# LRU branch ahead of GLA, one more Strassen pair, and other places for scans and cover, in a one-core encoder kernel

## The chip, the cores and the metric

One core of a Trainium2 chip runs the whole program. The metric is the time of one execution on the device in microseconds (us). The profile is of one execution; its span runs from the first instruction to the last. TensorE's matmul queue is called PE, VectorE DVE, ScalarE ACT; SP is the engine whose queue issues most transfers (DMA).

## What the kernel computes

784 tokens (16 meta tokens, 512 and 256 others) of width 2048 are normalised and projected by `w_in`. Three branches work on the columns, each runs over the tokens in both directions, and three sets of 2048 sigmoid gates merge them:

```python
cols = h @ w_in
u_a, gate_a, q_b, k_b, v_b, gate_b, glr_b, x_c, gate_c, merge = split_cols(cols)
y_a = s5_mixer(u_a, ...) * silu(gate_a)             # diagonal state space, 512 wide
y_b = gla_mixer(q_b, k_b, v_b, glr_b, ...) * silu(gate_b)   # gated attention in chunks, 4 heads
y_c = rglru_mixer(x_c, ...) * silu(gate_c)          # convolution, gates, scan, 1024 wide
gates = sigmoid(merge).reshape(bsz, length, 3, D_MODEL)
m = (gates[:, :, 0] * (y_a @ w_out_a) + gates[:, :, 1] * (y_b @ w_out_b)
     + gates[:, :, 2] * (y_c @ w_out_c))
return z + m @ w_o                                  # then a last rmsnorm
```

## The kernel before

Activations lie transposed: 16 tiles of 128 features by 784 tokens, each as a high part `h` and a low part `l` (names h_102, l_103 and so on). Weights are split likewise: `load_w` loads half a tile of 128 outputs (`raw`, 512 KB, two buffers), ACT copies the high part `hi` (L89), DVE subtracts for the low part `lo` (L61); `hi` and `lo` have three buffers each. Every product takes three matmuls (h·hi, l·hi, h·lo), for each half of the tokens. One output tile is thus 96 matmuls (16 x 3 x 2).

The order of the program is: start and projections of S5, branch S5, branch GLA, branch LRU, a Strassen phase (`strassen`, L1138) that computes merge gates and the branch gates in pairs of tiles, and the merge with the output products. The Strassen phase has 8 pairs for the branch gates and `NST` pairs for merge gates; a pair costs 168 matmuls for 2 tiles.

The other 48 - 2 `NST` tiles of merge gates are computed plainly, and most serve as filler for PE: `fill_step` (L273) does 6 of a tile's 96 matmuls and loads weights ahead, `cover(n)` does n such steps where it is called, and `tick` does them at a rate that `pace` sets. The rate is zero in GLA, LRU and behind them, so only `cover` fills there. What is left of the plain tiles is done at the head of `strassen`, between the calls of `sums`.

`sums(k)` (k from 0 to 7) loads two tiles (`xa` and `x`, two buffers each) of the normalised input from `xnorm` and forms the three sums of quadrants that Strassen's products need (`sh`, `sl`); `last_sum(k)` forms a fourth in the place of h and l. The loads for k = 0 and 1 are issued on ACT's queue, the others on SP's. The first products of the Strassen phase use the sums of k = 0 and 1.

In LRU, eight blocks n go through `conv`, `gates` (24 matmuls, L1051), `decays` and `scans`. Two blocks share the changes of ACT's function tables, so `decays` and `scans` are issued for a pair of blocks after each odd n. In GLA, `keys` and `queries` are projections (L199), the decays of a pair of heads come from the small matrix `glr` and the weights `wup` (L791), and attention ends with L916; normalisation of the heads follows (L935, sums over a tile of ones).

A scheduler in the framework sets the order of instructions on each engine when the kernel is built. On the chip each engine then runs in that order and waits where it must.

Of the kernel before, what the change touches and what calls it, by code (L numbers as in the profile page):

```python
# [6 lines left out]
F32 = mybir.dt.float32  # L7
# [7 lines left out]
NM, NP_, NS = 16, 512, 256  # L15
T = NM + NP_ + NS
# [3 lines left out]
HT = T // 2  # L20
# [3 lines left out]
SCRATCH = 1024  # L24
AHEAD = 6
SPLITN = 12
NST = 15
NA = 3
PREP = 6
WH = 3  # L30
PN = (1, 2)
XS = 2
LT = 39
MERGE0 = 36
GATES = [4, 5, 6, 7, 16, 17, 18, 19, 28, 29, 30, 31, 32, 33, 34, 35]
NG2 = len(GATES) // 2
# [59 lines left out]
def build(tc, A, out_p, out_s):  # L96
# [16 lines left out]
    first = S.dma_start(small[:], A["small"])  # L113
# [28 lines left out]
    psA = tc.alloc_tile_pool(name="psA", bufs=4, space=PSUM)  # L142
# [67 lines left out]
    def position(ci):  # L210

        return ci - sum(g < ci for g in GATES)
# [18 lines left out]

    merges = list(enumerate(MERGES[:48 - 2 * NST]))
    def merge_tile():
        i, (d, b) = merges.pop(0)
        merge_out(proj(MERGE0 + i, NM), d, b)
# [138 lines left out]
    ws = [load_w(A["w_in"][position(MERGE0), :, hk * 8:(hk + 1) * 8, :]) for hk in range(2)]  # L374
    for k in range(SPLITN, 16):
        normalise(k)
    pm = [bank(psA, "pm") for h in range(2)]
# [12 lines left out]
    E = dict(locals())  # L390
    branch_s5(E)
    pace(6)
    rates = lru_rates(V, col, cst, gp)
    first = branch_gla(E)
    pace(7)
    branch_lru(E, first, *rates)
    yh, yl = strassen(E)
    gp.release()

# [9 lines left out]
def branch_s5(E):  # L409
    tc, A = E["tc"], E["A"]  # L410
    V, S, PE, SP = E["V"], E["S"], E["PE"], E["SP"]
    col, split, proj, tick, pace, psB, drm, ident, ud = (E[k] for k in (
        "col", "split", "proj", "tick", "pace", "psB", "drm", "ident", "ud"))
# [5 lines left out]
        out=o, in0=x, scalar1=s1, scalar2=s2, op0=o0, **({"op1": o1} if o1 is not None else {}))  # L419
# [111 lines left out]
    for i in range(2):  # L531
        for j in range(4):
            d = 1 - j // 2
            a = Ap[:, 8, i, d * NG:(d + 1) * NG]
# [134 lines left out]
    for q in range(63):  # L669
        if q < 31:  # L670
            advance(33 + q, 34 + q, 1, 3)
        elif q == 31:
            advance(33 + q, 34 + q, 1, 2)
        else:
            advance(q - 31, q - 30, 0, 3)
        tick()
    pace(3)
    for e in range(NE):
        if e + 2 < NE:
# [10 lines left out]
    for n in range(4):  # L690
# [7 lines left out]
        t = fp.tile([128, NT], F32, name="ft")  # L698
# [6 lines left out]
        h = fp.tile([128, NT], F32R, name=f"fh{n}", bufs=1)  # L705
# [8 lines left out]
    for m in range(4):  # L714
# [6 lines left out]
        for h in range(2):  # L721
            sl = slice(h * HN, (h + 1) * HN)
            ps = psB.tile([128, 512], F32, name="br")
# [10 lines left out]
    fp.release()  # L734


def branch_gla(E):
    tc, A = E["tc"], E["A"]
    V, S, PE, SP = E["V"], E["S"], E["PE"], E["SP"]
    col, split, proj, evac, tick, psB = (E[k] for k in ("col", "split", "proj", "evac", "tick", "psB"))  # L740
# [11 lines left out]
    def tmp():  # L752
        return lp.tile([128, T], F32, name="tmp", bufs=4)

    qsp, qip, am = [], [], []
    for i in range(2):
        t = lp.tile([128, 2, 2, 128], F32, name=f"qsp{i}")
        V.memset(t[:], 0.0)
        qsp.append(t)
        t = lp.tile([128, 2, 2, 128], F32, name=f"qip{i}")  # L760
        V.memset(t[:], 0.0)
        qip.append(t)
        t = lp.tile([128, 2, 2, 128], F32, name=f"am{i}")
# [4 lines left out]
    def keys(hp):  # L768
        t = lp.tile([128, T], F32, name="kk")
        evac(t[:], proj(10 + hp, 0), 0)  # L770
        return t

    def queries(hp):
        t = lp.tile([128, NT], F32, name="qq")
        evac(t[:], proj(8 + hp, NM), NM, scale=0.125)
        return t

    kk, qq = keys(0), queries(0)
    S.table("natural_log_exp_and_others")
    for hp in range(2):  # L780

# [3 lines left out]
        for d in range(2):  # L785
            ab = tmp()
            zm = tmp()
            for h in range(2):
                sl = slice(h * HT, (h + 1) * HT)
                ps = psB.tile([128, 512], F32, name="br")  # L790
# [24 lines left out]
        for h in range(2):  # L815
            for g0, blks in ((0, (0, 1, 2, 3)), (4, (4, 5, 6))):
                ps = psB.tile([128, 512], F32, name="br")
# [13 lines left out]
        dec = lp.tile([128, 2, NTL], F32, name="dec")  # L831
        S.activation(out=dec[:, 0, :], in_=bc[:, 0, 143:T:128], func=AF.Exp, scale=IG)
        S.activation(out=dec[:, 1, :], in_=bc[:, 1, 16:T:128], func=AF.Exp, scale=IG)
        for d in range(2):
# [12 lines left out]
            ps = psB.tile([128, 512], F32, name="br")  # L847
# [4 lines left out]
            if d == 0:  # L852
                ps = psB.tile([128, 512], F32, name="br")
                PE.transpose(ps[:16, 0:128], kd[:, 0:16], ident[:])
                S.copy(out=kt[:16, 4, :], in_=ps[:16, 0:128])
                ps = psB.tile([128, 512], F32, name="br")
# [6 lines left out]
            for b in order:  # L863
                ps = psB.tile([128, 512], F32, name="br")
                PE.matmul(ps[:, :256], kt[:, reg.index(b), :], vt[:, b, :, :], start=True, stop=True)
                t = b - 1
# [14 lines left out]
        for t in range(NTL):  # L881
            qs, qi, a = qsp[it % 2], qip[it % 2], am[it % 2]
# [37 lines left out]
        for h in range(2):  # L920
            o = oo[:, h, :]
            sq = tmp()[:, :NT]
            S.activation(out=sq[:], in_=o, func=AF.Square)
            if hp == 0 and h == 0:
                kk = keys(1)
            elif hp == 0:
                qq = queries(1)
            elif h == 0:
                first = proj(20, 0)
            v = tmp()[:, :NT]  # L930
            r = tmp()[:, :NT]
            for i in range(2):
                sl = slice(i * HN, (i + 1) * HN)
                ps = psB.tile([128, 512], F32, name="br")
                PE.matmul(ps[:, :HN], ones[:], sq[:, sl], start=True, stop=True)  # L935
                V.tensor_scalar(out=v[:, sl], in0=ps[:, :HN], scalar1=1.0 / 128, scalar2=EPS,
                                op0=ALU.mult, op1=ALU.add)
            S.activation(out=r[:], in_=v[:], func=AF.Ln)
            S.activation(out=r[:], in_=r[:], func=AF.Exp, scale=-0.5)
            E["rsqrt_newton"](r[:], v[:], sq[:])  # L940
            V.scalar_tensor_tensor(out=o, in0=o, scalar=col("gla_g", 2 * hp + h), in1=r[:], op0=ALU.mult, op1=ALU.mult)
            S.dma_start(E["hspill"][4 + 2 * hp + h], o)
            tick()
    lp.release()
    return first


def exp_acc(V, out, x, r, k, ki):
# [36 lines left out]
    return cp, cn  # L985


def branch_lru(E, first, cp, cn):
    tc, A = E["tc"], E["A"]
    V, S, PE, SP = E["V"], E["S"], E["PE"], E["SP"]  # L990
    col, split, proj, evac, tick, psB = (E[k] for k in ("col", "split", "proj", "evac", "tick", "psB"))
    psA = E["psA"]
    XW, CW, HC = 808, 804, 402

    ws = []

    def load_half(ci, hk):

        if ci < 28:
            ws.append(E["load_w"](A["w_in"][E["position"](ci), :, hk * 8:(hk + 1) * 8, :]))  # L1000
        elif hk == 0:
            E["fill_ahead"]()

    def half(ps, hk):
        E["proj_mm"](ps, *ws.pop(0), hk, 0, HT)

    lp = tc.alloc_tile_pool(name="lp", bufs=1, reuse_waits="tile")

# [63 lines left out]
    def scans(n, gate, a):  # L1072
        for d in range(2):
            gi = gate[2 * d + 1]
            V.tensor_tensor(out=gi[:], in0=gi[:], in1=gate[2 * d][:], op=ALU.mult)
            if d == 0:
                hf = lp.tile([128, CW], F32, name="hf")
                for lo, hi in ((0, 528), (531, 803)):
                    V.tensor_tensor_scan(out=hf[:, lo:hi], data0=a[0][:, lo:hi], data1=gi[:, lo:hi], initial=0.0,
                                         op0=ALU.mult, op1=ALU.add)  # L1080
            else:
                hb = lp.tile([128, NT], F32, name="hb", bufs=2)
                for lo, hi, o in ((16, 528, 0), (547, 803, 512)):
                    V.tensor_tensor_scan(out=rev(hb[:, o:o + hi - lo]), data0=rev(a[1][:, lo:hi]),
                                         data1=rev(gi[:, lo:hi]), initial=0.0, op0=ALU.mult, op1=ALU.add)
            tick()
        V.tensor_tensor(out=hb[:, :512], in0=hb[:, :512], in1=hf[:, 16:528], op=ALU.add)
        V.tensor_tensor(out=hb[:, 512:], in0=hb[:, 512:], in1=hf[:, 547:803], op=ALU.add)
        S.dma_start(E["hspill"][8 + n], hb[:])

    load_half(21, 0)
    ready = conv(0, first)
    pair = []
    for n in range(8):
        if n < 7:
            ps = [E["bank"](psA, "pm") for h in range(2)]
            half(ps, 0)
            load_half(21 + n, 1)
        if n % 2 == 0:
            S.table("sigmoid_and_others")  # L1100
        pair.append((n, gates(n, *ready)))
        if n < 7:
            half(ps, 1)
            load_half(22 + n, 0)
            ready = conv(n + 1, ps)
        if n == 7:
            E["cover"](LT)
        if n % 2:
            S.table("exp_and_others")
            dec = [decays(m, g) for m, g in pair]  # L1110
            S.table("sqrt_and_others")
            for m, g in pair:
                for d in (0, 2):
                    S.activation(out=g[d][:], in_=g[d][:], func=AF.Sqrt)
            for (m, g), a in zip(pair, dec):
                scans(m, g, a)
            pair = []
    lp.release()


def weight_sums(V, r, t):
# [427 lines left out]
def strassen(E):  # L1549
# [78 lines left out]
    xp = tc.alloc_tile_pool(name="stu", bufs=1, reuse_waits="tile")  # L1628
    for i in range(NG2 + NST):
        ps = {j: next_bank() for j in (1, 2, 3, 6, 7, 5, 4)}  # L1630
        for sb in range(4):
            products(PE, ps, ahead.pop(0), sb, 8, operand)
            n = 4 * i + sb + 1
            if n > 2 and n < 4 * (NG2 + NST):
                ahead.append(weights(*divmod(n, 4)))
# [6 lines left out]
        if i < NG2:  # L1642
# [9 lines left out]
            continue  # L1652
        for g, (d, b) in zip((g1, g2), MERGES[48 - 2 * NST + 2 * (i - NG2):]):
            S.dma_start(E["gspill"][d, :, b, :], g[:])
# [29 lines left out]
def layout(inp):  # L1684
# [7 lines left out]
    order = [36 + 16 * b + d for d, b in MERGES]  # L1692
    std = order[:48 - 2 * NST]
    D["w_in"] = np.ascontiguousarray(w3[[i for i in range(36) if i not in GATES] + std])
    pairs = GATES + order[48 - 2 * NST:]
    st = []
# [88 lines left out]
```

## Time and profile before

| what | value |
|---|---|
| median of 3 runs | 2044.0 us (2043.46 to 2046.32) |
| the profiled execution | 2045.25 us, its span 2043.4 us |
| PE busy | 2005.7 us (98%) |
| DVE busy | 1503.8 us (74%) |
| ACT busy | 806.7 us (39%) |
| mean granted clock of TensorE | 0.995 of full |

Busy shares are shares of the span. The profile gives the end of a matmul longer than the distance to the next one, since matmuls overlap; so what PE needs for a run of them is read from start to start.

### The profile page before, as it was taken

To read this page: it belongs to the slowest core of one execution; us is meant where nothing else is said; L and a number is where in the kernel's file an instruction comes from. 1 tells how busy PE (TensorE), PEld (TensorE's weight loads), DVE (VectorE), ACT (ScalarE), POOL (GpSimd) and SP (SyncE) were. 2 spreads that over 40 slices of the span, in tenths; PEclk is the share of its full clock that TensorE was granted. 3 is DMA by queue.
4 is the path that set the end of the run, shared out by engine and by line. 5 is a ranking of instruction groups with operands and counts; after the bars stand their busy time and mean duration, and the time that the engine had idled before them with its cause. 6 is when DMAs were issued, how large, how long until landed. Compare 5 with 4: busy or idle time off the path is not lost.

```text
span 2043.4 us, 30984 instructions
## 1 busy us (share of the span) xinstructions
PE 2005.7 (98%) x12228; PEld 1975.6 (97%) x12228; DVE 1503.8 (74%) x2784; ACT 806.7 (39%) x1172; POOL 0.2 (0%) x4
## 2 busy tenths in 40 slices
PE   8999989999999999999999999999999999999997
PEld 8999989999999999999999999999999999999997
DVE  8988983746567875876776656655669989887778
ACT  7332111433437765433333222222235435533345
POOL 0000000000000000000000000000000000000000
PEclk9999989999999999999999999999999999999999
DMA  8652224521211223533443233323356335532256
GB/s 292 253 120 93 75 91 117 173 65 34 75 34 63 90 83 108 181 125 113 135 134 111 88 104 103 104 88 104 104 176 221 124 112 182 173 120 94 94 162 218
DMA packets 105378, 252.12 MB, mean 123 GB/s; under 512 B 18960, under 2 KB 39952, under 8 KB 105232
## 3 DMA queue, kind: packets, MB, share of 16 engines
q1 hardware_dynamic: 77072, 200.61, 30.6%
q10 hardware_dynamic: 28160, 49.53, 6.8%
q8 instruction: 96, 1.57, 0.3%
q14 instruction: 50, 0.41, 0.1%
HBM read 200.65 MB, written 49.45 MB: 122 GB/s over the span
## 4 chain that ended last, share of the span: by engine, by line
PE 86%; DVE 9%; ACT 3%; DMA 2%; issue 0%; SPq 0%; DVEq 0%; ACTq 0%
PE pm L1138 24%; PE br L1138 23%; PE pm L199 13%; PE pm L273 9%; PE br L1411 4%; PE pm L1281 2%; PE br L1281 2%; DVE sc L61 2%; PE pm L332 2%; DVE W L61 2%; PE br L1051 1%; DVE lo L61 1%; DMA c<-gspill 1%; PE br L199 1%; PE pm L1411 1%; ACT gt L89 1%
## 5 line engine op out<-in xcount | busy, mean ns | idle before, releaser
L89 ACT ACTIVATE hi<-raw 128x768 fp32r<-128x768 f32 (+2 forms) x234 | 216.0, 923 | 493.1 <-PE br L1138 131.5
L61 DVE TENSOR_TENSOR lo<-raw,hi 128x768 fp32r<-128x768 f32 (+2 forms) x234 | 246.1, 1053 | 141.2 <-ACT hi L89 141.1
L61 DVE TENSOR_TENSOR lo<-t,hi 128x1024 fp32r<-128x1024 f32 x140 | 171.4, 1224 | 193.9 <-ACT hi L89 193.8
L89 ACT ACTIVATE hi<-t 128x1024 fp32r<-128x1024 f32 x140 | 148.4, 1060 | 281.7 <-PE pm L1138 135.4
L1138 PE MATMUL pm<-l,hi 128*128 128x384 f32 (+1 forms) x616 | 197.3, 320 | 0.0
L1138 PE MATMUL pm<-h,hi 128*128 128x384 f32 (+1 forms) x616 | 196.6, 319 | 0.0
L1138 PE MATMUL pm<-h,lo 128*128 128x384 f32 (+1 forms) x616 | 196.6, 319 | 0.0
L1138 PE MATMUL br<-l,hi 128*128 128x384 f32 (+1 forms) x504 | 167.0, 331 | 0.0
L1138 PE MATMUL br<-h,hi 128*128 128x384 f32 (+1 forms) x504 | 165.9, 329 | 0.0
L1138 PE MATMUL br<-h,lo 128*128 128x384 f32 (+1 forms) x504 | 165.8, 329 | 0.0
L199 PE MATMUL pm<-h,hi 128*128 128x392 f32 (+1 forms) x608 | 162.2, 345 | 1.2 <-ACT xp L1020 1.2
L199 PE MATMUL pm<-h,lo 128*128 128x392 f32 (+1 forms) x608 | 159.1, 341 | 2.5 <-DVE lo L61 2.5
L199 PE MATMUL pm<-l,hi 128*128 128x392 f32 (+1 forms) x608 | 159.7, 341 | 0.0
L273 PE MATMUL pm<-h,hi 128*128 128x384 f32 x512 | 134.1, 343 | 0.0
L273 PE MATMUL pm<-h,lo 128*128 128x384 f32 x512 | 132.1, 339 | 2.1 <-DVE lo L61 2.1
L273 PE MATMUL pm<-l,hi 128*128 128x384 f32 x512 | 132.6, 340 | 0.0
L1138 PEld LDWEIGHTS pm<-h,hi 128*128 128x128 f32 x616 | 115.7, 188 | 0.4 <-ACT h L89 0.2
L1138 PEld LDWEIGHTS pm<-h,lo 128*128 128x128 f32 x616 | 116.0, 188 | 0.0
L1138 PEld LDWEIGHTS pm<-l,hi 128*128 128x128 f32 x616 | 115.7, 188 | 0.0
L199 PEld LDWEIGHTS pm<-h,lo 128*128 128x128 f32 x608 | 111.2, 188 | 2.8 <-DVE lo L61 2.8
L199 PEld LDWEIGHTS pm<-h,hi 128*128 128x128 f32 x608 | 111.1, 188 | 2.8 <-ACT xp L1020 1.5
L199 PEld LDWEIGHTS pm<-l,hi 128*128 128x128 f32 x608 | 110.6, 188 | 0.2
(358 smaller groups left out, 4802.2 us busy)
## 6 DMA issues: line engine op xcount, KB each, us to landing
raw<-in_w_st SPq DMA_DIRECT2D x92, 512.0 KB
raw<-in_w_in SPq DMA_DIRECT2D x74, 512.0 KB
gspill<-g ACTq DMA_DIRECT2D x48, 384.0 KB
raw<-in_w_ost SPq DMA_DIRECT2D x32, 512.0 KB
xr<-in_xT SPq DMA_DIRECT2D x31, 392.0 KB
m<-gspill SPq DMA_DIRECT2D x26, 384.0 KB
raw<-in_w_out SPq DMA_DIRECT2D x16, 512.0 KB
raw<-in_w_outc SPq DMA_DIRECT2D x16, 512.0 KB
```

The lines of the kernel that those rows point to most:

```text
L61: return f(*a, **k)
L89: ins = self.eng.activation(**k)
L199: PE.matmul(ps[h][:, :nw], w[:, k, :], xx[kt][:, n0 + h * nw:n0 + (h + 1) * nw], start=(kt == 0 and j == 0), stop=(kt == 15 and j == 2))
L273: PE.matmul(ps[h][:, :HN], w[:, k % 8, :], xx[k][:, NM + h * HN:NM + (h + 1) * HN], start=(k == 0 and j == 0), stop=(k == 15 and j == 2))
L332: PE.matmul(ps0[2 * t + h][:, :HT], w[:, k, :], xx[kt][:, h * HT:(h + 1) * HT], start=(kt == 0 and j == 0), stop=(kt == 15 and j == 2))
L1051: PE.matmul(ps[:, :HC], w[:, gs], xx[:, sl], start=(j == 0), stop=(j == 2))
L1138: PE.matmul(ps[j][:, :nt], w[:, wi, kk, :], x, start=(k == 0 and q == 0), stop=(k == n - 1 and q == 2))
L1281: PE.matmul(ps[h][:, :HN], w[:, 4 * b + k, :], yy[4 * b + k][:, h * HN:(h + 1) * HN], start=(k == 0 and j == 0), stop=(k == 3 and j == 2))
L1411: PE.matmul(po[:, :NS], x[:, n, :], y[k][:, ss], start=(first and j == 0), stop=(last and j == 2))
```

## The change

Branch LRU runs ahead of GLA. `NST` goes from 15 to 16. LRU's last block, which had 39 steps of cover (`LT`) behind it, gets GLA's first keys and queries instead (`next_branch`, 192 matmuls into tiles of a pool `kq`); GLA's last head, which had LRU's first projection (96 matmuls) beside it, gets `cover(16)` (also 96). LRU's first projection `proj(20, 0)` is now called at its own start. In S5, `cover(6)` (36 matmuls) is called behind the loop of `advance`. In LRU the scans of a pair of blocks are issued one at a time: the first after the odd block, the second after the next even one.

```diff
-NST = 15
+NST = 16
-LT = 39
...
-    first = branch_gla(E)
+    kq = tc.alloc_tile_pool(name="kq", bufs=1)
+    first = branch_lru(E, kq, *rates)
     pace(7)
-    branch_lru(E, first, *rates)
+    branch_gla(E, *first)
+    kq.release()
     yh, yl = strassen(E)
...
         tick()
+
+    E["cover"](6)
     pace(3)
...
-    kk, qq = keys(0), queries(0)
...
             elif h == 0:
-                first = proj(20, 0)
+                E["cover"](16)
...
+    def next_branch():
+
+        out = []
+        for i, (ci, n0, scale) in enumerate(((10, 0, 1.0), (8, NM, 0.125))):
+            ps = [E["bank"](psA, "pm") for h in range(2)]
+            load_half(ci, 1)
+            half(ps, 0, n0)
+            if i == 0:
+                load_half(8, 0)
+            half(ps, 1, n0)
+            t = kq.tile([128, T - n0], F32, name=("kk0", "qq0")[i])
+            evac(t[:], ps, n0, scale=scale)
+            out.append(t)
+        return out
...
+    first = proj(20, 0)
     load_half(21, 0)
     ready = conv(0, first)
...
         if n == 7:
-            E["cover"](LT)
-        if n % 2:
+            first = next_branch()
+        if n % 2 == 0:
+            scan_one()
+        else:
...
-            for (m, g), a in zip(pair, dec):
-                scans(m, g, a)
+            due = [(m, g, a) for (m, g), a in zip(pair, dec)]
+            scan_one()
             pair = []
+    scan_one()
```

Two places in the order of instructions carry most of what changes beside that.

The first is SP's queue where GLA's small inputs are loaded: `glr`, the masks and `wup`, among the loads of weights (`raw`). Before:

```order
L716 DMA fw<-in_w_glu 128x512 x2
L135 DMA raw<-in_w_in 128x1024 x4
L748 DMA glr<-glrd 64x784
L750 DMA masks<-in_gla_mask 128x256
L783 DMA wup<-in_gla_up 128x2x128
L135 DMA raw<-in_w_in 128x1024 x3
```

The same with the change, where `gw` are the weights of LRU's gates:

```order
L1038 DMA gw<-in_lru_w 128x512
L134 DMA raw<-in_w_in 128x1024 x7
L751 DMA glr<-glrd 64x784
L753 DMA masks<-in_gla_mask 128x256
L785 DMA wup<-in_gla_up 128x2x128
L134 DMA raw<-in_w_in 128x1024
```

The three loads now stand behind the seven weight loads that end LRU; the last two of these (named raw_6113 and raw_6425 in the full listing) take their buffers over from weights whose `lo` stands behind LRU's last scan on DVE.

The second is ACT's queue ahead of the Strassen phase, where `xa` and `x` for the first `sums` are loaded (`hb` is a result of LRU's scans, `g<-pm` empties a finished filler tile). Before:

```order
L1089 DMA hspill<-hb 128x768
L89 ACTIVATE g<-pm 128x384 x2
L89 ACTIVATE hi<-raw 128x1024
L240 DMA gspill<-g 128x768
L1089 DMA hspill<-hb 128x768
L1570 DMA xa<-xnorm 128x768
L1570 DMA x<-xnorm 128x384
L1570 DMA xa<-xnorm 128x768
L89 ACTIVATE hi<-raw 128x1024
L1570 DMA x<-xnorm 128x384
```

With the change, where `oo` is a head's result in GLA:

```order
L944 DMA hspill<-oo 128x768
L88 ACTIVATE hi<-raw 128x768
L88 ACTIVATE g<-pm 128x384
L1594 DMA xa<-xnorm 128x768
L1594 DMA x<-xnorm 128x384
L88 ACTIVATE g<-pm 128x384
L1594 DMA xa<-xnorm 128x768
L239 DMA gspill<-g 128x768
L88 ACTIVATE sh_7363<-x 128x384
L88 ACTIVATE sh_7367<-xa 128x384
L1594 DMA x<-xnorm 128x384
```

The first `xa` and `x` now stand behind `g<-pm`, which waits for the last filler tile but one to be finished, and the second `x` behind the first two `sh`. On PE, 438 filler matmuls (L273) stood between LRU's last gates and the first Strassen product; now 36, 20 and 172 (L272) stand between GLA's last attention matmul and that product, with two pairs of normalisation matmuls (L937) between them.

## Rows read from the trace of the kernel before

**Rows 1.** The page: busy time of the engines (share of the span), and the chain that ended last.
```profile
PE 2005.7 (98%) x12228; PEld 1975.6 (97%) x12228; DVE 1503.8 (74%) x2784; ACT 806.7 (39%) x1172; POOL 0.2 (0%) x4
PE 86%; DVE 9%; ACT 3%; DMA 2%; issue 0%; SPq 0%; DVEq 0%; ACTq 0%
```
**Rows 2.** PE's waits by releaser: us in total, times, longest us.
```profile
PE br L653 <- DVE W L61: 4.5, 1, 4.5
PE br L1051 <- ACT xch L89: 3.1, 2, 2.5
PE pm L199 <- DVE lo L61: 2.5, 1, 2.5
...
PE br L726 <- DVE fwl L61: 1.2, 1, 1.2
PE pm L199 <- ACT xp L1020: 1.2, 1, 1.2
```
**Rows 3.** Timeline of PE: cover between LRU's last gates and the Strassen phase.
```profile
772.21 0.51 PE L273 MATMUL pm<-h,hi 128*128 128x384 f32 x2
...
848.85 0.34 PE L1138 MATMUL br<-h,hi 128*128 128x384 f32 x1
```
**Rows 4.** Groups of PE's instructions from 769.1 to 848.8 us (one of three alike).
```profile
L273 PE MATMUL pm<-l,hi 128*128 128x384 f32 x146 | 37.5, 338 | 0.0
```
**Rows 5.** Timeline of PE in S5, at the end of the loop of advance.
```profile
279.54 0.46 PE L652 MATMUL br<-U,tp 128*128 128x96 f32 x2
284.47 0.74 PE L653 MATMUL br<-W,ca 128*128 128x96 f32 x2 [4.47 <-DVE W L61]
```
**Rows 6.** Windows of PE: span of it, busy us (instructions), granted clock, DMA.
```profile
765.90:767.50 1.60, 1.46 (x4) 0.50 0.00 0
...
284.40:289.10 4.70, 4.63 (x22) 0.50 0.46 146
289.10:290.50 1.40, 1.40 (x6) 0.50 0.87 244
...
667.80:669.00 1.20, 1.11 (x6) 1.00 0.17 27
```
**Rows 7.** Timeline of SP's queue: GLA's small loads.
```profile
389.11 0.53 SPq L748 DMA_DIRECT2D glr<-glrd  x1
...
401.76 0.61 SPq L783 DMA_DIRECT2D wup<-in_gla_up  x1
```
**Rows 8.** Timeline of PE: the first use of them.
```profile
424.23 2.79 PE L791 MATMUL br<-glr,wup 128*128 128x392 f32 x8
```
**Rows 9.** Timeline of DVE: end of LRU's scans, sums, first last_sum.
```profile
803.66 1.22 DVE L61 TENSOR_TENSOR lo<-raw,hi 128x1024 fp32r<-128x1024 f32 x1
...
811.58 0.56 DVE L61 TENSOR_TENSOR x<-x,xa 128x384 f32<-128x384 f32 x1 [6.71 <-DMA x<-xnorm]
...
819.59 0.56 DVE L61 TENSOR_TENSOR x<-x,xa 128x384 f32<-128x384 f32 x1 [0.94 <-DMA x<-xnorm]
...
843.32 0.69 DVE L61 TENSOR_TENSOR t<-raw 128x512 f32<-128x512 f32 x1
...
848.81 1.02 DVE L61 TENSOR_TENSOR l<-y,h 128x384 fp32r<-128x384 f32 x2
```
**Rows 10.** Groups of DVE's instructions from 812.0 to 843.3 us.
```profile
L61 DVE TENSOR_TENSOR x<-x,xa 128x384 f32<-128x384 f32 x16 | 8.6, 553 | 9.5 <-DMA x<-xnorm 9.5
...
L61 DVE TENSOR_TENSOR lo<-raw,hi 128x1024 fp32r<-128x1024 f32 (+1 forms) x4 | 4.6, 1152 | 0.0
```
**Rows 11.** Timeline of the queues of ACT and SP: loads for the sums.
```profile
806.54 0.45 ACTq L1570 DMA_DIRECT2D x<-xnorm  x1
...
816.12 0.38 SPq L1570 DMA_DIRECT2D x<-xnorm  x1
```
**Rows 12.** Timeline of PE: projection behind GLA's last attention matmul.
```profile
588.17 0.60 PE L199 MATMUL pm<-h,hi 128*128 128x392 f32 x2
...
594.70 1.45 PE L935 MATMUL br<-tmp,ones 128*128 128x384 f32 x4
```

More of the change, by code (lines that the diff above doesn't have):

```diff
@@ L734, in branch_s5, with branch_gla @@
     fp.release()
-def branch_gla(E):
+def branch_gla(E, kk, qq):
     tc, A = E["tc"], E["A"]
@@ L944, in branch_gla @@
     lp.release()
-    return first
 def exp_acc(V, out, x, r, k, ki):
@@ L985, in lru_rates, with branch_lru @@
     return cp, cn
-def branch_lru(E, first, cp, cn):
+def branch_lru(E, kq, cp, cn):
     tc, A = E["tc"], E["A"]
@@ L997, in load_half, with half @@
     def load_half(ci, hk):
[L999 to L1005, printed above, removed]
+        ws.append(E["load_w"](A["w_in"][E["position"](ci), :, hk * 8:(hk + 1) * 8, :]))
+    def half(ps, hk, n0=0):
+        E["proj_mm"](ps, *ws.pop(0), hk, n0, (T - n0) // 2)
+    def next_branch():
[11 more added lines that the diff above has]
+        return out
     lp = tc.alloc_tile_pool(name="lp", bufs=1, reuse_waits="tile")
@@ L1089, in scans, with scan_one @@
         S.dma_start(E["hspill"][8 + n], hb[:])
+    first = proj(20, 0)
     load_half(21, 0)
     ready = conv(0, first)
-    pair = []
+    pair, due = [], []
+    def scan_one():
+        if due:
+            scans(*due.pop(0))
     for n in range(8):
@@ L1103, in branch_lru @@
             half(ps, 1)
-            load_half(22 + n, 0)
+            load_half(22 + n if n < 6 else 10, 0)
             ready = conv(n + 1, ps)
         if n == 7:
-            E["cover"](LT)
-        if n % 2:
+            first = next_branch()
+        if n % 2 == 0:
+            scan_one()
+        else:
             S.table("exp_and_others")
@@ L1114, in branch_lru @@
                     S.activation(out=g[d][:], in_=g[d][:], func=AF.Sqrt)
-            for (m, g), a in zip(pair, dec):
-                scans(m, g, a)
+            due = [(m, g, a) for (m, g), a in zip(pair, dec)]
+            scan_one()
             pair = []
+    scan_one()
     lp.release()
+    return first
 def weight_sums(V, r, t):
```

## The prediction

> **What bounds the kernel.** I began with the page: PE is busy 2005.7 of 2043.4 us and holds 86% of the chain that ended last [rows 1]. So the time is PE's matmuls from start to start, plus the places where PE stands still. The list of PE's waits gives those places; it is short, and its largest entry is one pause of 4.5 us in S5 [rows 2]. The change can therefore gain in two ways only: fewer matmuls, or fewer pauses. It can lose by a new pause. For that I read, in the order of instructions, what stands behind what on each queue, and in the timelines how long the same work took before.
>
> The price of one matmul of a filler: from 772.21 to 848.85 us [rows 3] there are 438 of them (three groups of 146 [rows 4]), so 0.175 us each. In that stretch PE never waits: it is cover for two things at once, LRU's last scans and the eight `sums` that must be there before the Strassen products.
>
> **One more pair.** Two plain tiles (192 matmuls) become one Strassen pair (168): 24 fewer, 24 x 0.175 = 4.2 us less. The pair's additions on DVE lie in a phase where PE is the slower engine, so I cost them at nothing; they would show as waits of L1162 for DVE. **-4.2.**
>
> **`cover(6)` in S5.** PE stops at 279.54 plus two short matmuls and goes on at 284.47, waiting 4.47 us for DVE's W [rows 5]. When it comes back the granted clock is 0.50, that is 1.2 GHz, for the 4.7 us up to the next filler and for 1.4 us more [rows 6]; at the full clock this is half as long, so 2.35 + 0.7 us are lost beside the pause. The 36 matmuls of the cover are 36 x 0.175 = 6.3 us, longer than the pause, and their weights are split by then. Their number is not added to the program, only taken from a later place. **-7.5** (only -4.5 if the clock falls all the same).
>
> **Small pauses at the branches' edges.** L726 waits 1.2 us for DVE [rows 2]; now LRU's first projection (96 matmuls) stands ahead of it. LRU's start waits 1.2 us for ACT's `xp` [rows 2]; that place is now at the end of S5, with another projection beside it. I take **-1.3** and **-0.8** (zero at worst).
>
> **Scans one at a time.** Inside LRU, PE waits 2.5 us once for DVE's `lo` and 3.1 us in two pieces for `xch` [rows 2], both behind work on DVE. With one scan instead of two ahead of the next convolution the `lo` should be in time; the convolution's own chain (DVE, ACT, DVE, PE, ACT) is as long as before and still carries the loop. Between removing all of it with the slow clock behind one pause (-8) and an additional wait where a scan now stands ahead of another block's convolution (+3), I take the row of the `lo` less a little: **-2**.
>
> **From LRU to GLA.** Let G be the end of LRU's last gates; before it was 772.2 [rows 3]. DVE's tail ran up to 803.66 [rows 9], G + 31.5, with three `lo` in it at 1.15 us each [rows 10]; now there are two, so the scans end near G + 30.3. Then come two `lo` (G + 32.6), which free the buffers for the two last weight loads, and only behind these on SP's queue come `glr`, the masks and `wup`, each issue taking half a us and more [rows 7]: `wup` at about G + 33.9. A load of `x` was used 5.0 us after its issue in one place (806.54 to 811.58) and 3.5 us in another (816.12 to 819.59) [rows 9, 11], so `wup` is there at G + 37.4 to 38.9. PE gets to L793 after 197 matmuls of a projection; 36 of these took from 588.17 to 594.70, 0.18 us each [rows 12], so PE is there at G + 35.5. Before, `glr` was issued 35 us and `wup` 22 us ahead of that matmul [rows 7, 8]. The new pause is 2 to 3.4 us; I take 2.5, and 1 for the clock. Nothing but PE's own stream stands behind it, and GLA's chain starts as much later. **+3.5** (0 to 6).
>
> On the clock after such a pause the rows disagree: after 2.5 us ahead of L1051 it was 0.50, after 2.5 us ahead of L199 it was 1.00 [rows 2, 6]. The Trainium skill, "TensorE: Matmul & The Clock Gate", section "Why this matters for your kernels", warns of gaps between bursts of matmuls as what drops the clock. [...]
>
> **From GLA to the Strassen phase.** This is the large term. Let Q be the end of the last attention matmul, where the next projection's matmul starts (588.17 before [rows 12]). PE then has 36 + 20 + 172 fillers at 0.175 us and two times two matmuls of L937 (some 1.3 us each time, as an estimate from the 1.45 us of four records with their end [rows 12]): the first Strassen product starts at Q + 42.5. Its first 12 matmuls use the old h and l; the next ones, from Q + 44.6, need the sums and `last_sum(0)`. Before, PE had 76.6 us of cover here [rows 3], and l came at 848.81 + 0.5 = 849.3 [rows 9], just in time.
>
> Now, when does l come? ACT issues the first `xa` and `x` behind `g<-pm` of the last filler tile but one. That tile ends after 36 + 20 + 76 fillers and L937: 132 x 0.175 + 2.6 = Q + 25.7. A `hi`, one `g<-pm` and the issue of `xa` come first on ACT, 1.7 us as an estimate from the 1.15 us of a `lo` of like size [rows 10] and half of it, so `x` is issued at Q + 27.4. DVE starts the sums 5.0 us later [rows 9, 11], at Q + 32.4. From there to l it was 849.3 - 811.58 = 37.7 us, with four `lo` of fillers among it, 4.6 us [rows 10], which are no longer there: 33.1 us. So l comes at Q + 65.5 and PE stands for 65.5 - 44.6 = 20.9 us. DVE itself works only part of this: the sums go at the pace of two buffers of `x`, each loaded again only after its last use.
>
> Bounds: if the transfers never let DVE wait, 2.8 us of the idle time of `x<-x,xa` (9.5 less the first 6.71 [rows 9, 10]) fall away, and another 4 us if the first load lands at once: 14. If the second `x`, which now stands behind two `sh`, delays the next sums by 3 us, and the loads by as much again: 27. I stay with 21. After such a pause the clock should restart low: 6.1 us at 0.50 in S5 [rows 6] were a loss of 3; 2.5 here. **+23.5.**
>
> The Trainium skill has a price for the loads, "SBUF — State Buffer", section "The DMA setup-cost knee": about 2 us fixed and the bytes at 436 GB/s. By an estimate from that page an `x` of 192 KB takes 2.4 us where the rows have 3.5 to 5.0, and both new pauses would be 1 to 2.5 us shorter, with a sum some 4 us lower.
>
> **Sum.** -4.2 - 7.5 - 1.3 - 0.8 - 2 + 3.5 + 23.5 = +11.2. The profiled execution took 2045.25 us, 1.25 over the median of the runs shown; against the median the forecast is 2055.
>
> **Rivals.** (a) *Faster: no large pause ahead of the Strassen phase.* One mechanism: `x` and `xa` land much earlier than I say, since ACT's queue is not held up by the filler tile, and the sums run under GLA's tail. For it speaks that DVE has idle time there and that 42 us of cover remain. Against it speak ACT's static order and that one round of two sums took 8.0 us (811.58 to 819.59 [rows 9]). Without the pause the sum is 11.2 - 23.5 = -12.3: 2032. It decides from where l comes at Q + 54 or earlier: then the pause with its clock is 12 us and the whole change comes out even; at Q + 50 it is faster by 4. (b) *About even*: the pause exists but the loads are quick and LRU gives back most of its pauses, 14 + 1.5 and -6: sum near 0, 2042 to 2048. (c) *Worse*: the bounds of both edges together (27 + 3, 6) with LRU unchanged: -13.8 + 36 = +22, 2066.
>
> **Chances.** My forecast (2049 to 2061) 0.52; (a) 0.16; (b) 0.12; (c) 0.20. A change within 0.2%, 4 us, can't be told from none. Faster is 0.16, within 0.2% is 0.12, slower 0.72. The range reaches from the partly true (a) to (c): 2038 to 2067.
>
> **What would show it.** Right: 36 L272 ahead of L635 without a wait of L654 for W; a wait of 2 to 3 us of L793 for the load of `wup` or `glr`; a wait of about 20 us of L1162 for ACT's `hi` or DVE's l and for nothing else in that phase, with `x<-x,xa` waiting for DMA each round; clock at 0.50 behind it. Wrong: if the sums are found done before PE arrives, or if PE's new waits lie inside LRU or GLA, where I expect none over 3 us.

## The result and the profile after

The changed kernel takes 2057.0 us (median of 6 runs, 2054.45 to 2058.64); the kernel before took 2043.97 beside it. The ratio is 1.0059, 95% interval 1.0048 to 1.0070: it is 13 us slower. The profiled execution took 2056.76 us with a span of 2054.9.

The page of the changed kernel shows less work on PE and a smaller share of the chain that ended last (compare [rows 1]):

```profile
PE 2001.8 (97%) x12204; PEld 1969.7 (96%) x12204; DVE 1519.1 (74%) x2807; ACT 809.9 (39%) x1173; POOL 0.2 (0%) x4
...
PE 77%; DVE 13%; ACT 4%; DMA 4%; issue 2%; SPq 0%; ACTq 0%; DVEq 0%
```

There are 24 matmuls fewer, as there should be. What PE lost on the chain, DVE, ACT and DMA gained: other engines now decide the end for a while. PE's waits say where (columns as in [rows 2]):

```profile
PE br L1162 <- ACT hi L88: 17.4, 1, 17.4
PE pm L331 <- ACT hi L88: 5.8, 2, 5.5
PE br L793 <- DMA wup<-in_gla_up: 5.2, 1, 5.2
PE br L1064 <- ACT xch L88: 3.5, 3, 1.9
PE pm L272 <- DVE lo L60: 2.5, 2, 2.0
PE br L1162 <- DVE c L60: 1.5, 1, 1.5
PE br L729 <- DVE fwl L60: 1.2, 1, 1.2
```

The wait for W in S5 is gone, and so is the wait of a projection for DVE's `lo` in LRU. Two new ones stand at the edges between branches: 17.4 us of L1162 and 5.2 us of L793. L331 is the start of the program and waits alike in both kernels (5.6 us before); L729 still waits its 1.2 us, where I had expected none.

**The edge from GLA to the Strassen phase.** The timeline of PE:

```profile
769.82 0.60 PE L272 MATMUL pm<-h,hi 128*128 128x384 f32 x2
...
814.30 0.33 PE L1162 MATMUL br<-h,lo 128*128 128x384 f32 x1
832.01 0.69 PE L1162 MATMUL br<-sh,hi 128*128 128x384 f32 x1 [17.38 <-ACT hi L88]
```

and of the queue of ACT, then of DVE, for the same stretch:

```profile
795.61 0.33 ACTq L1594 DMA_DIRECT2D xa<-xnorm  x1
795.97 0.45 ACTq L1594 DMA_DIRECT2D x<-xnorm  x1
```

```profile
800.22 0.56 DVE L60 TENSOR_TENSOR x<-x,xa 128x384 f32<-128x384 f32 x1 [2.96 <-DMA x<-xnorm]
...
833.13 1.02 DVE L60 TENSOR_TENSOR l<-y,h 128x384 fp32r<-128x384 f32 x2
```

The last attention matmul ends where the next filler starts, at 769.8 (this is Q). `x` is issued at Q + 26.2 (forecast 27.4), the sums start at Q + 30.4 (32.4), and the first l is done at 833.6, Q + 63.8 (65.5). From the first sum to l it is 33.4 us, the forecast 33.1. DVE works in 29.7 of these 33.4 us; for loads of `x` it waits 4.9 us, of which 3.0 ahead of the first sum and 1.9 in three later places. Its window (us, busy us and instructions, clock, DMA) and its wait for `x` from 800 to 834 us:

```profile
800.20:833.60 33.40, 29.68 (x57) 0.78 0.53 165
```

```profile
DVE x L60 <- DMA x<-xnorm: 4.9, 4, 3.0
```

The twelfth product of the Strassen phase starts at 814.30; then PE stands until `hi` is there, which is made from the weights' sums just ahead of l.

**The edge from LRU to GLA.** SP's queue, and PE:

```profile
604.07 0.53 SPq L751 DMA_DIRECT2D glr<-glrd  x1
...
605.27 0.62 SPq L785 DMA_DIRECT2D wup<-in_gla_up  x1
```

```profile
571.74 0.52 PE L198 MATMUL pm<-l,hi 128*128 128x392 f32 x2
...
606.39 0.34 PE L198 MATMUL pm<-h,hi 128*128 128x392 f32 x1
611.88 0.99 PE L793 MATMUL br<-glr,wup 128*128 128x392 f32 x1 [5.15 <-DMA wup<-in_gla_up]
...
616.66 0.98 PE L198 MATMUL pm<-h,hi 128*128 128x392 f32 x1
```

The transfer, from the chain that ended last (start, us, what):

```profile
605.27 6.48 DMA wup<-in_gla_up
```

With G at 571.7 (the next projection's matmul behind LRU's last gates), `wup` was issued at G + 33.5 and PE came at G + 34.9, both within a us of the forecast. But `wup` landed only 6.5 us after its issue.

The granted clock behind both pauses, and in S5 where the pause was (columns as in [rows 6]):

```profile
284.00:292.00 8.00, 8.00 (x68) 1.00 0.46 146
611.90:617.30 5.40, 5.40 (x9) 0.50 0.10 36
832.00:835.80 3.80, 3.79 (x11) 0.50 0.69 231
```

In S5 the clock now stays at 1.00 where it was 0.50 [rows 6]. Behind the two pauses it is at 1.2 GHz for some 5.4 and 3.8 us.

### The profile page after: what moved, and what is told of

The parts are those of the page before. It is cut to its first block, busy times and chain, and to the rows that moved or that the text cites. A ratio compares the mean times of both kernels' runs of the same rounds, so it can differ in the third digit from the quotient of the medians.

```text
span 2054.9 us, 30979 instructions
## 1 busy us (share of the span) xinstructions
PE 2001.8 (97%) x12204; PEld 1969.7 (96%) x12204; DVE 1519.1 (74%) x2807; ACT 809.9 (39%) x1173; POOL 0.2 (0%) x4
## 4 chain that ended last, share of the span: by engine, by line
PE 77%; DVE 13%; ACT 4%; DMA 4%; issue 2%; SPq 0%; ACTq 0%; DVEq 0%
PE br L1162 23%; PE pm L1162 22%; PE pm L198 7%; PE pm L272 6%; PE pm L1435 3%; PE br L1305 2%; PE pm L1305 2%; DVE sc L60 2%; PE pm L331 2%; DVE W L60 1%; DVE lo L60 1%; PE br L1435 1%; ACT gt L88 1%; DVE xc L60 1%; DVE gt L60 1%
## 5 line engine op out<-in xcount | busy, mean ns | idle before, releaser
L1162 PE MATMUL pm<-l,hi 128*128 128x384 f32 (+1 forms) x576 | 187.9, 326 | 0.0
L1162 PE MATMUL br<-l,hi 128*128 128x384 f32 (+1 forms) x576 | 187.6, 326 | 0.1
L1162 PE MATMUL pm<-h,hi 128*128 128x384 f32 (+1 forms) x576 | 187.2, 325 | 0.0
L1162 PE MATMUL pm<-h,lo 128*128 128x384 f32 (+1 forms) x576 | 187.0, 325 | 0.0
L1162 PE MATMUL br<-h,lo 128*128 128x384 f32 (+1 forms) x576 | 186.5, 324 | 0.0
L1162 PE MATMUL br<-h,hi 128*128 128x384 f32 (+1 forms) x576 | 186.4, 324 | 0.0
L272 PE MATMUL pm<-h,hi 128*128 128x384 f32 x448 | 118.7, 345 | 0.0
L272 PE MATMUL pm<-h,lo 128*128 128x384 f32 x448 | 115.5, 338 | 2.5 <-DVE lo L60 2.5
L272 PE MATMUL pm<-l,hi 128*128 128x384 f32 x448 | 117.3, 342 | 0.0
L1162 PE MATMUL br<-sh,hi 128*128 128x384 f32 x288 | 96.7, 336 | 17.4 <-ACT hi L88 17.4
L198 PEld LDWEIGHTS pm<-l,hi 128*128 128x128 f32 x608 | 110.7, 188 | 0.3 <-issue 0.3
L1162 PEld LDWEIGHTS pm<-h,lo 128*128 128x128 f32 x576 | 108.8, 189 | 0.0
L1162 PEld LDWEIGHTS pm<-h,hi 128*128 128x128 f32 x576 | 108.4, 188 | 0.3 <-ACT h L88 0.2
```

Of the source, the lines that this page charges most:

```text
L198: PE.matmul(ps[h][:, :nw], w[:, k, :], xx[kt][:, n0 + h * nw:n0 + (h + 1) * nw], start=(kt == 0 and j == 0), stop=(kt == 15 and j == 2))
L272: PE.matmul(ps[h][:, :HN], w[:, k % 8, :], xx[k][:, NM + h * HN:NM + (h + 1) * HN], start=(k == 0 and j == 0), stop=(k == 15 and j == 2))
L1162: PE.matmul(ps[j][:, :nt], w[:, wi, kk, :], x, start=(k == 0 and q == 0), stop=(k == n - 1 and q == 2))
```

## Experiments

All times are medians. Each run was timed beside the kernel before on the same chip, which took 2044.66 us in the first four runs and 2044.41 in the last three; ratios are to that. A difference between the changed kernel and another version is that of their medians; by the ratios it would be 0.4 to 0.7 us larger. The new order of the branches was not run by itself.

**The pair undone (e1).**

```diff
-NST = 16
+NST = 15
```

> The changed kernel with NST back at 15, all else as changed: 24 more matmuls (+4.2 us), and 192 more fillers (33.5 us) between GLA's last attention and the first Strassen product. Theory A (the loss is the pause ahead of the Strassen phase, since the fillers there run out before the sums are made): the pause of 17.4 us and the slow restart (2.5 us) go away, 2057 + 4.2 - 20 = 2041 us (2038 to 2044). Rival B (the loads for the sums stand behind a filler tile, so more tiles push them back as well): the pause stays near 17 us, 2061 us.

2040.58 us, ratio 0.9980 [0.9972, 0.9989], as Theory A said. PE has one wait of L1162 left, of 0.3 us: with two more filler tiles it comes to the Strassen phase later than the sums. This is where DVE makes the first l, in the timeline of DVE, and where PE uses it, in that of PE:

```profile
837.96 0.55 DVE L60 TENSOR_TENSOR l<-y,h 128x384 fp32r<-128x384 f32 x1
```

```profile
847.66 0.34 PE L1162 MATMUL pm<-l,hi 128*128 128x384 f32 x1
```

It is done at 838.5, so some 9 us are in hand. The `x` loads did not move back with the tiles (the first is issued at 795.21, at 795.97 in the changed kernel), so rival B is out. The pair, which saves 4.2 us of matmuls, cost 2057.0 - 2040.6 + 4.2 = 20.6 us at this edge.

**The small loads on GpSimd's queue (e2).**

```diff
-    SP.dma_start(glr[:64, :], E["glrd"][:])
+    E["nc"].gpsimd.dma_start(glr[:64, :], E["glrd"][:])
...
-        SP.dma_start(wup[:], A["gla_up"][:, :, hp * 128:(hp + 1) * 128])
+        (SP if hp else E["nc"].gpsimd).dma_start(wup[:], A["gla_up"][:, :, hp * 128:(hp + 1) * 128])
```

> The changed kernel, with glr and the first wup loaded on GpSimd's queue instead of behind the weights on SP's. Theory A (the pause of L793 is the late place in SP's queue): the wait of 5.2 us falls below 1 us and the matmuls of L793 run at the full clock, 7 to 8 us less than the changed kernel, about 2049 us. Rival B (the buffers that the two tiles take over come free late, or the transfer is slow whatever its queue): 2 us or less is gained, 2055 to 2057 us.

2049.82 us, ratio 1.0022 [1.0012, 1.0032], 7.2 us less than the changed kernel, as Theory A said. `wup` is issued at 576.5, and this is its time to landing:

```profile
DMA to landing us min/median/max: 3.0/3.0/3.0
```

PE goes through L793 without a wait and at the full clock:

```profile
608.40 2.79 PE L793 MATMUL br<-glr,wup 128*128 128x392 f32 x8
610.73 0.82 PE L198 MATMUL pm<-h,lo 128*128 128x392 f32 x2
```

Eight records in 2.79 us, as before ([rows 8]). L1162 still waits 16.8 us: what was gained at the first edge was not eaten at the second. The buffers were thus free 29 us earlier; it was the place in SP's queue that held the loads, and behind the weights there the transfer of `wup` took twice as long as well (6.5 us against 3.0).

**The cover in S5 alone, on the kernel before (e4).**

```diff
         tick()
+
+    E["cover"](6)
     pace(3)
```

> The kernel before with cover(6) behind the loop of advance in S5, and nothing else changed. Theory A (the pause of 4.5 us for W and its slow restart are all that stands there): 7.5 us less, 2036.5 us. Rival B (36 fillers are missing later and the wait shows up at another place): 2 us less or no gain, 2042 to 2044 us.

2039.76 us, ratio 0.9976 [0.9967, 0.9985]: 4.9 us less, between the two. The wait for W is gone. But the fillers come so close behind each other that the first of them waits for its own weights, 0.46 us in the timeline of PE:

```profile
279.70 0.62 PE L273 MATMUL pm<-h,lo 128*128 128x384 f32 x2 [0.46 <-DVE lo L61]
```

and a second pause, 0.7 us at L728, opens near the end of S5, beside the one of 1.2 us that stays there. What S5 itself gained can be read where PE leaves its loop, at the first filler behind it: before, in this run, and in the changed kernel:

```profile
346.32 0.60 PE L273 MATMUL pm<-h,hi 128*128 128x384 f32 x2
```

```profile
349.81 0.60 PE L273 MATMUL pm<-h,hi 128*128 128x384 f32 x2
```

```profile
349.82 0.60 PE L272 MATMUL pm<-h,hi 128*128 128x384 f32 x2
```

By then 912 fillers are done before, and 972 in the other two. The 60 more are 10.5 us of work, and PE is only 3.5 us later: S5 is 7.0 us shorter in both. In this run part of it is lost again in LRU, where the same wait of 2.5 us for `lo` as before [rows 2] is followed by a clock of 0.50, where it was 1.00 [rows 6]:

```profile
662.60:665.90 3.30, 3.30 (x12) 0.50 0.80 248
```

That costs some 1.7 us in the profiled execution, far behind the edit; why the clock fell there and not before is not shown. So the mechanism is A's, and in S5 nearly its size too.

**The pair alone, on the kernel before (e5).** The diff is the change of NST from 15 to 16.

> The kernel before with NST 16 alone. 24 matmuls fewer (-4.2 us), 192 fillers fewer ahead of the Strassen phase. Theory A (cover is what the pair costs): PE is at the first use of the sums 33.5 us earlier, the sums come at most 4 us earlier (fewer weights to split), so a pause of 27 to 32 us and a slow restart of 2.5: 2069 to 2074 us. Rival B (the sums were late only because fillers slowed them): a pause under 10 us, 2042 to 2050 us.

2066.58 us, ratio 1.0108 [1.0095, 1.0122]. PE's longest wait:

```profile
PE br L1138 <- ACT hi L89: 23.3, 1, 23.3
```

So the pause does not belong to the new order of the branches: the pair opens it in the old order as well, and there it is longer. It is below my 27 to 32 us, since the first l was done at 842.3, 7 us earlier than before ([rows 9]) and not 4: besides the `lo` of fillers that are no longer in the sums' way, the first sum began 1.8 us earlier (809.83), and the second round followed after 6.9 us instead of 8.0. The first l in DVE's timeline:

```profile
841.76 1.02 DVE L61 TENSOR_TENSOR l<-y,h 128x384 fp32r<-128x384 f32 x2
```

**Scans of a pair together (e6).**

```diff
-        if n % 2 == 0:
-            scan_one()
-        else:
+        if n % 2:
...
             scan_one()
+            scan_one()
             pair = []
-    scan_one()
```

> The changed kernel with the scans of a pair of blocks issued together behind the odd block, as before. Theory A (one scan at a time is what took the wait of 2.5 us for DVE's lo out of LRU): the wait comes back, 2059 to 2060 us. Rival B (the order of branches and the weights loaded half a tile earlier took it out): no difference, 2056 to 2058 us.

2056.25 us, ratio 1.0060 [1.0047, 1.0072], the same as the changed kernel. The wait of a projection for DVE's `lo` does not come back; PE's waits in LRU are these, beside 3.5 and 1.2 in the changed kernel:

```profile
PE br L1064 <- ACT xch L88: 4.1, 3, 2.3
...
PE br L1064 <- DVE xcl L60: 1.2, 2, 0.6
```

Theory A is out. What removed the wait for `lo`, the weights loaded half a tile earlier or the new order of the branches, is left open; neither was tried by itself.

**The first loads for the sums on SP's queue (e7).**

```diff
-XS = 2
+XS = 0
```

> The changed kernel with the loads of xa and x for k = 0 and 1 on SP's queue, not on ACT's. Theory A (ACT's queue, behind the filler tile's g, holds the sums up): the first loads are issued some 4 us earlier (behind a weight load at 791.4), the pause of L1162 is 13 to 14 us, 2053 us. Rival B (the buffers that xa and x take over come free only then, or SP's queue stands just as late): the pause stays at 17 us, 2057 us.

2054.3 us, ratio 1.0048 [1.0035, 1.0060], 2.7 us less than the changed kernel; the intervals overlap, so the finding rests on the trace. The first `x` is issued at 792.1 (795.97 before that edit), but is in use only 6.2 us later; the first l is done 2.7 us earlier:

```profile
830.41 1.02 DVE L60 TENSOR_TENSOR l<-y,h 128x384 fp32r<-128x384 f32 x2
```

and PE's pause is 14.8 us, where Theory A had 13 to 14:

```profile
829.28 0.69 PE L1162 MATMUL br<-sh,hi 128*128 128x384 f32 x1 [14.81 <-ACT hi L88]
```

ACT's queue does hold the sums up, by some 2.6 us of pause; the other 14.8 us are the sums themselves, DVE's work for the most part, for which PE has too little cover.

**Both edges mended (e9): NST 15 and the small loads on GpSimd's queue.** The diffs are those of e1 and e2.

> The changed kernel with NST 15 and with glr and the first wup on GpSimd's queue: both pauses at the edges removed together. Theory A (the two pauses are separate and all that the change loses): 2040.6 less the 7.2 us that GpSimd's queue gave, 2033.5 us (2031 to 2036), under the kernel before and under every other version here. Rival B (one gain is hidden behind the other): 2038 to 2041 us.

2033.06 us, ratio 0.9945 [0.9931, 0.9958], as Theory A said: 11 us less than the kernel before and 24 less than the changed one, with no wait over 0.6 us at either edge. It is the fastest version of this study.

## Why the prediction was right

The forecast was 2055, slower, by two pauses at the edges of GLA; measured were 2057.0 and those two pauses. The mechanism was right in the main. That the number came within 2 us is in part luck: the first edge cost 3.7 us more than its term and the second 2.9 us less.

- **The Strassen edge (+23.5).** Undoing the pair gives 20.6 us back there. The steps were right to 2 us each: arrival of PE, issue of the loads, start and length of the sums. The pause was 17.4 us and not 20.9 for two reasons. `x` was issued 1.2 us earlier, while the `hi` ahead of it was still running on ACT (795.43 to 796.28), where I had added the work of ACT to its issue, and it was in use after 4.3 us instead of 5.0. And PE stood for `hi`, 1.6 us ahead of the end of l. The length of the sums was right because it came from the row before; the reason that I gave for it, the pace of the two buffers of `x`, was not. DVE works in 29.7 of the 33.4 us, and the sign "waiting for DMA each round" was not met: three waits, 1.9 us together. I had weighed the price for a load in the Trainium skill ("SBUF — State Buffer", "The DMA setup-cost knee"), by which the pause would be shorter. The load of `x` took 4.3 us from issue to use, nearer to my row than to the 2.4 us of the estimate; the measurement decides.
- **From LRU to GLA (+3.5).** The mechanism was right and the size half of what came: e2 measured 7.2 us. The late term was the transfer. I had it land 3.5 to 5.0 us after its issue, by the rows of `x`; it took 6.5 us right behind the weight loads, and 3.0 on another queue 29 us earlier. So the wait was 5.2 us and not 2 to 3; with 3.0 us at its late place it would, by an estimate, have been 1.6 (605.27 + 3.0 - 606.7). The clock then cost 2.5 us in L793 alone (4.8 us from start to start, 2.3 in e2), where I had put 1.
- **S5 (-7.5).** The clock is at 1.00 in that stretch now, as forecast, and S5 is 7.0 us shorter, in e4 as in the changed kernel. "Their weights are split by then" failed for one of them, 0.46 us. That the time of e4 fell by 4.9 us alone has its reasons behind S5's loop: the new wait at L728 and the clock in LRU.
- **Small pauses (-1.3, -0.8).** The first did not come: L729 waits 1.2 us as L726 did, and 0.6 us more for ACT. The second, LRU's start, is gone from the list of waits.
- **LRU (-2).** PE's waits there fell from 2.5 + 3.1 + 0.6 + 0.4 to 3.5 + 1.2 us. The reason I gave, one scan instead of two, is refuted by e6. The clock of 0.50 behind the longest of these waits [rows 6] is gone too, but in e2 it is there again; why is not shown, and no term of the forecast stands for it.
- **The pair (-4.2).** 24 matmuls fewer, as counted.

With the measured sizes, -4.2 - 7.0 + 7.2 + 20.6 is +16.6; 13.0 were measured, so 3.6 us were gained in the rest, LRU and the small pauses, where the forecast had 4.1 (1.3 + 0.8 + 2). What made up these 3.6 us was not taken apart by runs. A check that uses none of these sizes: e9 has neither the pair nor the two pauses and is 11.4 us faster than the kernel before, and the terms for S5, the small pauses and LRU add up to 11.6. That bears out their sum, not each of them.

Rival (a), no large pause, had its turning point at l by Q + 54; it came at Q + 63.8. Rival (c) was not far: one of its two bounds, 6 us at the first edge, was in fact passed.

## What to carry to other kernels

Filler that "only" covers has a price when it is spent: before a plain tile is turned into a cheaper form, count what must be ready when the filler ends, and how long that takes from the event that starts it; 33.5 us of filler bought 4.2 us of matmuls here and cost 20.6. When two stages change places, follow the small loads at a stage's head through their queue: they inherit whatever now stands in front of them, and a queue of their own (7.2 us here) is cheap. And an edit that removes a pause is worth testing with the others left out: the best version here is the changed kernel without its pair and with two small loads on another queue.

## What the runs showed of the hardware

- A load of 131 KB (`wup`) landed 6.5 us after its issue behind weight loads on SP's queue, while 230 GB/s were moved, and in 3.0 us on GpSimd's queue, in a stretch with 153 GB/s.
- The granted clock after a pause is not a matter of its length alone in these rows: after two waits of 2.5 us it was 0.50 once and 1.00 once [rows 2, 6], and the second of these, ahead of L199, was followed by 0.50 in e4. A wait of 1.9 us ahead of L1064 was followed by 1.00 in the changed kernel and by 0.50 in e2. After 5.2 and 17.4 us it was 0.50 both times, for some 5.4 and 3.8 us, so the longer pause did not cost the slower restart. So 1 to 2 us between two profiled executions can come from the clock alone.
